# Where the softmax denominators of a head pair are transposed: from a PSUM bank of their own to the free block of the weights' bank, one step later

## The chip, the cores and the metric

The kernel runs on one core of a Trainium2 chip. The metric is the time of one execution on the device in microseconds (us). Engines work side by side, each in its own order: TensorE (PE in the profile; PEld is its weight load, which overlaps its matmuls), VectorE (DVE), ScalarE (ACT), GpSimd (POOL) and SyncE (SP, which here only issues DMAs; SPq is its queue). They wait for one another by semaphores. Matmuls and transposes on TensorE write to PSUM, which has eight banks of 128 partitions by 512 fp32 values; ScalarE and VectorE read them out.

## The reference

One layer of an encoder on 512 positions of width 1024, all in fp32:

```python
h = rms_norm(x, g1)
xr, gate, q, k, v = split(h @ w_in)
y_rnn  = (rg_lru(conv(xr), forward) + rg_lru(conv(xr), backward)) * gelu(gate)
y_attn = dilated_attention(q, k, v, rel_bias)     # 8 heads of 64
x = x + concat(rms_norm(y_rnn, ga), rms_norm(y_attn, gb)) @ w_out
x = x + square(relu(rms_norm(x, g2) @ w_up)) @ w_down
return rms_norm(x, g3)
```

The change is in `dilated_attention`. Each head looks at its keys through three windows (128 wide in steps of 1, 512 in steps of 4, 2048 in steps of 16), each with a softmax of its own, and the three outputs are combined by their denominators:

```python
lse = logsumexp(logits_w)                  # for each window w
out_w = softmax(logits_w) @ v
y = sum_w softmax_over_windows(lse)_w * out_w
```

This equals one softmax over the union of the keys, where a key that lies in several windows counts as often. So one sum of exponentials per query and head is enough, and the output is the weighted sum of values times the reciprocal of that sum, the denominator.

## The kernel before, in words

Matrix products are done in three passes with operands split into a high and a low part (`mm3`, lines 317 to 319). Weights stream in as chunks of 128 x 1024: a DMA brings a chunk to `wraw` (line 235), ScalarE makes the high part `whi` (line 252), VectorE the low part `wlo` (line 274), three chunks ahead of TensorE.

The positions are held by parity and half, in four query tiles of 128. Attention goes over four pairs of heads. The loop at line 1170 has five rounds, i = 0 to 4, of four steps, u = 0 to 3. In round i it computes the logits and exponentials of pair i (where i < 4), and transposes the exponentials of pair i - 1 (where i > 0). One step does, in this order on TensorE:

- `att_s` (line 815): the logits of one query tile for both heads of pair i, in two banks `ps` of the tag `gs` (four matmuls, line 824).
- `att_t` for both heads of pair i - 1 (line 857): three 128 x 128 transposes (line 862) of the exponentials `e` into one bank `pt`, of the tag `et`, which has two banks in turn; then ScalarE copies the three blocks to `ett` (line 865). A bank has room for four blocks. The key tile `jt` needs four query tiles, but of the fourth only 32 columns are inside the windows; `att_c` (line 867) does these on VectorE. The block left free in `pt` is block 0 for even `jt` and block 3 for odd `jt`. The step number u is the `jt` of the call.
- `att_e` (line 826), on VectorE and ScalarE: bias and row minimum (line 840), then the exponential with its sum (line 841), which adds up the denominators in `zz`.
- fillers: matmuls of the next projections (`pqk`) or of the output projection (`pwo`), in four places of a step, as `FILL` says.

When the four tiles of `ett` of a pair are there, `att_av` (line 961) multiplies them with the values into the bank `pav`, and line 976 multiplies by the reciprocal denominators `zrow`.

Those come in four parts. `att_z(i - 1)`, in step 0 of round i, takes the reciprocals on VectorE (line 892) and spreads each over 16 columns of a 128 x 128 tile `z16` (line 894; the profile names it `z`). `att_zt` (line 896), in the same step before the last place for fillers, transposes `z16` with TensorE into a bank `prow`, taken from the two banks of the tag `et` (line 898), and ScalarE copies it back over `z16` (line 899). `att_zd` (line 901), in step 1, after the second place for fillers, issues four DMAs from SP (line 906) that spread the rows of `z16` over `zrow`.

The order of the instructions on TensorE, ScalarE, VectorE and GpSimd is that of the program; this is set at line 112. SP is not in that list: the order of its DMAs, and which buffer of a tag a new tile gets, come from the planner that places the tiles. Tiles like `z16`, `ett`, `e` and `zrow` share one pool of 45 buffers (`g_`, line 118).

Of the kernel before, what the change touches and what calls it, by code (L numbers as in the profile page):

```python
# [14 lines left out]
AF = mybir.ActivationFunctionType  # L15
OP = mybir.AluOpType

P = 128
# [85 lines left out]
def hybrid_kernel(ctx: ExitStack, tc, xw0, xw, xn, w_in, w_v, w_out, w_up, w_dn, gates, vecs, rel, onehot, fg, out):  # L104
    nc = tc.nc
# [8 lines left out]
    act = nc.scalar.activation  # L114
# [3 lines left out]
    def g_(name, dt=FT, shape=(P, S)):  # L118
        return work.tile(list(shape), dt, name=name, tag="g", bufs=NG)
# [4 lines left out]
    def ps_(name, tag):  # L124
        return psum.tile([P, S], FT, name=name, tag=tag, bufs={"pj": 4, "gs": 2, "et": 2}[tag])
# [12 lines left out]
    ident = consts.tile([P, P], FT, name="ident")  # L138
# [268 lines left out]
    def fan(t, c, n, w):  # L407
        base = t[:, c:c + 1]
        return bass.AP(tensor=base.tensor, offset=base.offset, ap=[base.ap[0]] + ([[1, n]] if n > 1 else []) + [[0, w]])
# [77 lines left out]
    def load_tw(h, v):  # L487
        t = work.tile([P, 1024], FT, name="tw", tag="tw", bufs=4)[:, :2 * WN + TH + P]
        b = nbd.offset + h * 2 * S
        nc.sync.dma_start(t[:, WN:WN + TH + P], bass.AP(tensor=nbd.tensor, offset=b, ap=[[1, P], [1, TH + P]]))  # L490
        k = TH - WN - v
        nc.sync.dma_start(bass.AP(tensor=t.tensor, offset=t.offset, ap=[t.ap[0], [WN + TH + P, 2], [1, WN]]),
                          bass.AP(tensor=nbd.tensor, offset=b + S + k, ap=[[1, P], [P - 1 + v - k, 2], [1, WN]]))
        tws[h, v] = t
# [312 lines left out]
    et, en, zs = {}, {}, {}  # L807
# [7 lines left out]
    def att_s(p, u):  # L815
        qt = QSEQ[u]
        par, far = QT[qt]
        c0 = P * qt
        w = {(0, 0): TH + TH - WN, (0, 1): 0, (1, 0): TH - WN, (1, 1): TH}[par, far]
        psq[p] = [ps_("ps", "gs") for _ in range(2)]  # L820
        for e in range(2):
            k = k_tile(p, e)[:, w:w + NK]
            for i, n in enumerate(("h", "l")):
                nc.tensor.matmul(psq[p][e][:, :NK], lhsT=sp[p, 0, n, e][:, c0:c0 + P], rhs=k, start=i == 0, stop=i == 1)  # L824

    def att_e(p, u):
        qt = QSEQ[u]
        par, far = QT[qt]
        v = int(par != far)
        if u == 0:  # L830
            en[2 * p], en[2 * p + 1] = {}, {}
            zs[p] = small("zz", 8)
        pss = psq.pop(p)
        c0 = (WN + P) * far
        for e in range(2):
            h = 2 * p + e
            t = g_("e")
            mn = small("mn", 1)
            x = t[:, :NK] if far else t[:, S - NK:]
            nc.vector.tensor_tensor_reduce(x, pss[e][:, :NK], tws[h, v][:, c0:c0 + NK], 1.0, 3.0e38, OP.add, OP.min, mn)  # L840
            act(x, x, AF.Exp, scale=-1.0, bias=mn, accum_out=zs[p][:, 2 * qt + e:2 * qt + e + 1])
            en[h][qt] = t
            if u in (1, 3):
                del tws[h, v]
        if u == 3:
            for e in range(2):
                del sp[p, 0, "h", e], sp[p, 0, "l", e], sp[p, 1, "h", e]
            del kks[p]


    def blocks(jt):
        par, hj = jt // 2, jt % 2
        own = [(2 * (1 - par) + a, (P * hj if a else TH + P * hj)) for a in range(2)]
        oth = [(2 * par + a, (TH + P * hj if a else P * hj)) for a in range(2)]
        return (own + oth, slice(0, NK)) if hj else (oth + own, slice(S - NK, S))

    def att_t(h, jt):
        pt = ps_("pt", "et")
        bs = list(enumerate(blocks(jt)[0]))
        bs.pop(3 if jt % 2 else 0)  # L860
        for i, (qt, k) in bs:
            nc.tensor.transpose(pt[:, i * P:(i + 1) * P], en[h][qt][:, k:k + P], ident)  # L862
        t = et[h, jt] = g_("ett")
        c = slice(bs[0][0] * P, (bs[2][0] + 1) * P)
        act(t[:, c], pt[:, c], AF.Copy)

    def att_c(h, jt):
        hj = jt % 2
        qt = blocks(jt)[0][3 if hj else 0][0]
        c = slice(NK - 32, NK) if hj else slice(S - NK, S - NK + 32)  # L870
        nc.vector.transpose(et[h, jt][:, c], en[h][qt][:, c])
        if jt == 3:
            del en[h]
# [9 lines left out]

    pav, zrow = {}, {}

    z16 = {}

    def att_z(p):  # L890
        rz = small("rz", 8)
        nc.vector.reciprocal(rz, zs.pop(p))
        z16[p] = g_("z16")[:, :P]
        nc.vector.tensor_copy(z16[p], fan(rz, 0, 8, 16))

    def att_zt(p):
        pr = ps_("prow", "et")
        nc.tensor.transpose(pr[:, :P], z16[p], ident)
        act(z16[p], pr[:, :P], AF.Copy)

    def att_zd(p):
        zrow[p] = g_("zrow")
        t = z16.pop(p)
        for qt in range(4):
            r = t[32 * qt:32 * qt + 32]
            nc.sync.dma_start(zrow[p][:, qt * P:(qt + 1) * P],
                              bass.AP(tensor=r.tensor, offset=r.offset, ap=[r.ap[0], [0, 4], [1, P]]))

    def att_y(p):
        y_add(1)  # L910
# [50 lines left out]
    def att_av(p, jts):  # L961
        if 0 in jts:
            pav[p] = ps_("pav", "gs" if p else "pj")
        for jt in jts:
            parts = av_parts(jt)
            for i, (ci, co) in enumerate(parts):
                for e in range(2):
                    a = slice(64 * e, 64 * e + 64)
                    h = 2 * p + e
                    nc.tensor.matmul(pav[p][a, co], lhsT=vs[:, jt, h * DH:(h + 1) * DH], rhs=et[h, jt][:, ci],  # L970
                                     start=jt == 0 and i == 0, stop=jt == 3 and i == len(parts) - 1, skip_group_check=True)
            for e in range(2):
                del et[2 * p + e, jt]
        if 3 in jts:
            y = g_("yp")
            nc.vector.tensor_tensor(y[:, ::-1], pav.pop(p), zrow.pop(p), op=OP.mult)
            yat[p] = y
            if p == 3:
                att_a(p)
            if p != 2:  # L980
                att_q(p)
            if p < 2:
                att_a(p)
# [64 lines left out]
    def fill(n):  # L1048
        for _ in range(n):
            if fillers and fillers[0] is None:  # L1050
                fillers.popleft()
                load_x()
            if fillers:
                fillers.popleft()()
# [8 lines left out]
    def add_x():  # L1063
        for fn in more.popleft() if more else ():
            fn()
# [83 lines left out]
    def beside(*key):  # L1149
        for e in plan.pop(key, ()):  # L1150
            e()
# [18 lines left out]
    for i in range(5):  # L1170
        for u in range(4):
            if i < 4:
                att_s(i, u)
                if u == 2 and i < 3 or u == 0 and i:
                    for e in range(2):
                        load_tw(2 * (i + u // 2) + e, u // 2)
            if i >= 1:
                att_t(2 * i - 2, u)
                att_t(2 * i - 1, u)
            if i < 4:  # L1180
                att_e(i, u)
            if i >= 1:
                att_c(2 * i - 2, u)
                att_c(2 * i - 1, u)
            if u == 0 and i >= 1:
                att_z(i - 1)
            if u == 0:
                for p in AVS.get(i, ()):
                    att_av(p, range(4))
            beside(i, u, 0)  # L1190
            fill(FILL.get((i, u), (1, 1, 1, 1))[0])
            beside(i, u, 1)
            fill(FILL.get((i, u), (1, 1, 1, 1))[1])
            if u == 1 and i >= 1:
                att_zd(i - 1)
            if u == 0:
                for p in AVS.get(i, ()):
                    if p != 2:
                        att_y(p)
            beside(i, u, 2)  # L1200
            fill(FILL.get((i, u), (1, 1, 1, 1))[2])
            beside(i, u, 3)
            if u == 0 and i >= 1:
                att_zt(i - 1)
            fill(FILL.get((i, u), (1, 1, 1, 1))[3])
            add_x()
            beside(i, u, 4)
# [339 lines left out]
    for half in range(2):  # L1547
# [202 lines left out]
        if half == 1:  # L1750
# [27 lines left out]
            pr = ps_("pd", "pj")  # L1778
# [63 lines left out]
```

## Time and profile before

| | |
|---|---|
| median of 3 runs | 531.06 us (530.21 to 531.57) |
| the profiled execution: its time | 530.99 us |
| its span, first to last instruction | 528.9 us |
| mean granted TensorE clock | 0.998 |
| TensorE busy | 521.5 us, 99% of the span |
| VectorE, ScalarE busy | 437.5 us (83%), 357.2 us (68%) |
| attention rounds 1 to 4, from the trace | about 110 to 176 us of the span |

A row of the timeline gives the start in the span, the time from the first start to the last end of the instructions in the row, the engine, the source line, the operation with its output and inputs, the shape and the count; in brackets, how long the engine sat idle before it and what ended that. Matmuls overlap: the time that one takes from the engine is the distance of its start to the next one's start, not the duration in its row. The chain of waits gives this more directly: each row is the start, the time that the chain spent there, and on what. The list of waits gives engine, tile and line, what was waited for, and then the total, the number of times and the longest.

### The profile page before, as it was taken

To read this page: it belongs to the slowest core of one execution; us is meant where nothing else is said; L and a number is where in the kernel's file an instruction comes from. 1 tells how busy PE (TensorE), PEld (TensorE's weight loads), DVE (VectorE), ACT (ScalarE), POOL (GpSimd) and SP (SyncE) were. 2 spreads that over 40 slices of the span, in tenths; PEclk is the share of its full clock that TensorE was granted. 3 is DMA by queue.
4 is the path that set the end of the run, shared out by engine and by line. 5 is a ranking of instruction groups with operands and counts; after the bars stand their busy time and mean duration, and the time that the engine had idled before them with its cause. 6 is when DMAs were issued, how large, how long until landed. Compare 5 with 4: busy or idle time off the path is not lost.

```text
span 528.9 us, 8275 instructions
## 1 busy us (share of the span) xinstructions
PE 521.5 (99%) x3003; PEld 448.0 (85%) x3003; DVE 437.5 (83%) x672; ACT 357.2 (68%) x578; POOL 66.0 (12%) x89
## 2 busy tenths in 40 slices
PE   9999999999999999999999999999999999999995
PEld 7856888877887788899999888888999999888884
DVE  5999888987886888898779986879756988987885
ACT  6578947788865757586477755575566777655664
POOL 0272000000000041001200312001101210232000
PEclk9999999999999999999999999999999999999999
DMA  8654286587588289948395899986978397799704
GB/s 284 210 165 141 81 227 189 161 238 207 134 293 286 60 167 210 377 134 227 97 220 145 218 270 274 309 299 147 280 219 220 105 217 213 168 300 260 182 1 159
DMA packets 42600, 107.02 MB, mean 202 GB/s; under 512 B 4916, under 2 KB 15284, under 8 KB 42560
## 3 DMA queue, kind: packets, MB, share of 16 engines
q1 hardware_dynamic: 34848, 80.14, 46.1%
q0 software_dynamic: 7536, 26.14, 26.7%
q8 instruction: 23, 0.38, 0.3%
q10 hardware_dynamic: 176, 0.23, 0.1%
q14 instruction: 17, 0.14, 0.1%
HBM read 94.92 MB, written 4.23 MB: 187 GB/s over the span
## 4 chain that ended last, share of the span: by engine, by line
PE 96%; DMA 1%; DVE 1%; issue 1%; ACT 0%; SPq 0%; DVEq 0%; ACTq 0%
PE pu L317 10%; PE pu L318 10%; PE pu L319 10%; PE pd L317 10%; PE pd L318 10%; PE pd L319 10%; PE pwo L317 3%; PE pqk L317 3%; PE pwo L319 3%; PE pwo L318 3%; PE pqk L319 3%; PE pqk L318 3%; PE pav L970 2%; PE ps L824 2%; PE pt L862 2%; PE pv L317 2%
## 5 line engine op out<-in xcount | busy, mean ns | idle before, releaser
L274 DVE TENSOR_TENSOR wlo<-wraw,whi 128x1024 fp32r<-128x1024 f32 x71 | 86.7, 1221 | 24.5 <-ACT whi L252 24.2
L252 ACT ACTIVATE whi<-wraw 128x1024 fp32r<-128x1024 f32 x67 | 70.8, 1059 | 36.5 <-PE pd L319 19.3
L318 PE MATMUL pd<-wlo,ah 128*128 128x512 f32 (+1 forms) x195 | 75.2, 386 | 0.0
L317 PE MATMUL pd<-whi,ah 128*128 128x512 f32 (+1 forms) x195 | 75.2, 386 | 0.0
L319 PE MATMUL pd<-whi,al 128*128 128x512 f32 (+1 forms) x195 | 75.2, 386 | 0.0
L252 ACT ACTIVATE whi<-tw 128x1024 fp32r<-128x1024 f32 x38 | 40.2, 1059 | 40.7 <-DMA tw<-in_w_up_dram 12.9
L318 PE MATMUL pu<-hl,whi 128*128 128x256 f32 x224 | 63.4, 283 | 0.0
L319 PE MATMUL pu<-hh,wlo 128*128 128x256 f32 x224 | 63.4, 283 | 0.0
L317 PE MATMUL pu<-hh,whi 128*128 128x256 f32 x224 | 63.4, 283 | 0.0
L274 DVE TENSOR_TENSOR wlo<-tw,whi 128x1024 fp32r<-128x1024 f32 x38 | 46.4, 1221 | 18.7 <-ACT whi L252 18.6
L317 PE MATMUL pu<-h2h,whi 128*128 128x256 f32 (+1 forms) x200 | 60.1, 300 | 0.0
L318 PE MATMUL pu<-h2l,whi 128*128 128x256 f32 (+1 forms) x200 | 60.0, 300 | 0.0
L319 PE MATMUL pu<-h2h,wlo 128*128 128x256 f32 (+1 forms) x200 | 60.0, 300 | 0.0
L317 PEld LDWEIGHTS pu<-hh,whi 128*128 128x128 f32 x224 | 43.0, 192 | 0.0
L318 PEld LDWEIGHTS pu<-hl,whi 128*128 128x128 f32 x224 | 43.0, 192 | 0.0
L319 PEld LDWEIGHTS pu<-hh,wlo 128*128 128x128 f32 x224 | 43.0, 192 | 0.0
L319 PEld LDWEIGHTS pd<-whi,al 128*128 128x128 f32 x195 | 36.6, 188 | 7.4
L317 PEld LDWEIGHTS pd<-whi,ah 128*128 128x128 f32 x195 | 36.6, 188 | 7.3
L318 PEld LDWEIGHTS pd<-wlo,ah 128*128 128x128 f32 x195 | 36.6, 188 | 7.3
L252 ACT ACTIVATE whi<-ts 128x1024 fp32r<-128x1024 f32 x24 | 25.5, 1061 | 23.9 <-PE pd L319 18.1
L317 PEld LDWEIGHTS pu<-h2h,whi 128*128 128x128 f32 x200 | 38.3, 191 | 1.3
L319 PEld LDWEIGHTS pu<-h2h,wlo 128*128 128x128 f32 x200 | 38.3, 191 | 1.3
(282 smaller groups left out, 1250.3 us busy)
## 6 DMA issues: line engine op xcount, KB each, us to landing
wraw<-in_w_up_dram SPq DMA_DIRECT2D x25, 512.0 KB, 5.5
ts<-in_w_dn_dram POOLq DMA_DIRECT2D x24, 512.0 KB, 13.3
wraw<-in_w_dn_dram SPq DMA_DIRECT2D x24, 512.0 KB, 7.1
tw<-in_w_up_dram SPq DMA_DIRECT2D x15, 512.0 KB, 5.4
tw<-in_w_up_dram POOLq DMA_DIRECT2D x15, 512.0 KB, 8.4
wraw<-in_w_in_dram SPq DMA_DIRECT2D x13, 512.0 KB, 3.6
ts<-in_w_dn_dram SPq DMA_DIRECT2D x8, 512.0 KB, 6.6
tw<-in_w_dn_dram SPq DMA_DIRECT2D x8, 512.0 KB, 6.1
```

Of the source, the lines that this page charges most:

```text
L252: act(hi, raws[i], AF.Copy)
L274: nc.vector.tensor_tensor(lo, r, f(splits[i][0]), op=OP.subtract)
L317: nc.tensor.matmul(o, lhsT=a[0], rhs=b[0], start=bool(first), stop=False, skip_group_check=on)
L318: nc.tensor.matmul(o, lhsT=a[0], rhs=b[1], start=False, stop=False, skip_group_check=on)
L319: nc.tensor.matmul(o, lhsT=a[1], rhs=b[0], start=False, stop=bool(last), skip_group_check=on)
L824: nc.tensor.matmul(psq[p][e][:, :NK], lhsT=sp[p, 0, n, e][:, c0:c0 + P], rhs=k, start=i == 0, stop=i == 1)
L862: nc.tensor.transpose(pt[:, i * P:(i + 1) * P], en[h][qt][:, k:k + P], ident)
L970: nc.tensor.matmul(pav[p][a, co], lhsT=vs[:, jt, h * DH:(h + 1) * DH], rhs=et[h, jt][:, ci], start=jt == 0 and i == 0, stop=jt == 3 and i ...
```

## The change

`att_zt` and its call go. In `att_t`, for the first head of the pair (`h % 2 == 0`) and `jt == 1`, the tile `z16` of this pair is transposed into block 3 of `pt`, after the three blocks of exponentials; after ScalarE's copy of the three blocks, a second copy takes block 3 back to `z16`. That is the first `att_t` of step 1 in place of the end of step 0. `att_z` and `att_zd` stay where they are in the program.

```diff
+    z16 = {}
+
     def att_t(h, jt):
         pt = ps_("pt", "et")
         bs = list(enumerate(blocks(jt)[0]))
         bs.pop(3 if jt % 2 else 0)
+        z = z16[h // 2] if (h % 2, jt) == (0, 1) else None
         for i, (qt, k) in bs:
             nc.tensor.transpose(pt[:, i * P:(i + 1) * P], en[h][qt][:, k:k + P], ident)
+        if z is not None:
+            nc.tensor.transpose(pt[:, 3 * P:], z, ident)
         t = et[h, jt] = g_("ett")
         c = slice(bs[0][0] * P, (bs[2][0] + 1) * P)
         act(t[:, c], pt[:, c], AF.Copy)
+        if z is not None:
+            act(z, pt[:, 3 * P:], AF.Copy)
...
-    def att_zt(p):
-        pr = ps_("prow", "et")
-        nc.tensor.transpose(pr[:, :P], z16[p], ident)
-        act(z16[p], pr[:, :P], AF.Copy)
...
             beside(i, u, 3)
-            if u == 0 and i >= 1:
-                att_zt(i - 1)
             fill(FILL.get((i, u), (1, 1, 1, 1))[3])
```

More of the change, by code (lines that the diff above doesn't have):

```diff
@@ L884, in hybrid_kernel @@
     pav, zrow = {}, {}
-    z16 = {}
     def att_z(p):
```

## The prediction

> **What bounds the kernel now.** I read the page first (busy shares, clock, the chain by engine), then TensorE's list of waits, then the four places where the lone transpose stands, in the timeline and in the chain of waits, and last the queues beside them.
>
> ```profile
> span 528.9 us, 8275 instructions
> PE 521.5 (99%) x3003; PEld 448.0 (85%) x3003; DVE 437.5 (83%) x672; ACT 357.2 (68%) x578; POOL 66.0 (12%) x89
> ...
> PE 96%; DMA 1%; DVE 1%; issue 1%; ACT 0%; SPq 0%; DVEq 0%; ACTq 0%
> ```
>
> TensorE is the bound: busy for 99% of the span, 96% of the chain. Time on another engine counts only where TensorE then waits. Little of its time is waiting, but two entries of its list belong to the step that is moved:
>
> ```profile
> PEld prow L898 <- issue: 0.8, 1, 0.8
> ...
> PEld pt L862 <- ACT z L899: 0.6, 2, 0.3
> ```
>
> The first is the lone transpose in one round: TensorE stands before it. The second is twice a batch of `pt` transposes that waits until ScalarE has read `prow`, since that tile took one of the two `et` banks out of turn.
>
> **The change part by part.** Counts do not change: four transposes of `z` and four copies of 128 x 128 go, four of each come; reciprocals and the 16 DMAs stay. What counts is where they stand.
>
> *The transpose itself.* Its price on the path, alone (rounds 2, 3, 4) and in a batch of six (round 2), from the chain of waits:
>
> ```profile
> 134.87 0.11 PE prow L898
> ...
> 136.43 0.65 PE pt L862 x6
> ...
> 151.73 0.11 PE prow L898
> ...
> 170.29 0.11 PE prow L898
> ```
>
> Alone it takes 0.11 us; in a batch 0.65 / 6 = 0.11. So moving it gains and costs nothing by itself: 4 x (0.11 - 0.11) = 0.
>
> *The wait in round 1.* TensorE and VectorE there, then two later batches for comparison:
>
> ```profile
> 113.21 0.40 PE L319 MATMUL pqk<-h_hi,wlo 128*128 128x512 f32 x1
> 113.95 0.30 PE L898 MATMUL prow<-ident,z 128*128 128x128 f32 x1 [0.35 <-DVE z L894]
> 114.01 0.48 PE L317 MATMUL pqk<-h_hi,whi 128*128 128x512 f32 x1
> 114.33 0.39 PE L318 MATMUL pqk<-h_lo,whi 128*128 128x512 f32 x1
> 114.56 0.39 PE L319 MATMUL pqk<-h_hi,wlo 128*128 128x512 f32 x1
> ...
> 115.55 1.08 PE L862 MATMUL pt<-ident,e 128*128 128x128 f32 x6
> ...
> 112.65 0.59 DVE L840 CUSTOM_DVE_ANT_0 e<-ps,tw 128x416 f32<-128x416 f32 x1 [1.29 <-issue]
> ...
> 113.58 0.23 DVE L894 COPY z<-rz 128x128 f32<-128x128 f32 x1
> ...
> 136.27 0.82 PE L862 MATMUL pt<-ident,e 128*128 128x128 f32 x6
> ...
> 170.24 1.08 PE L862 MATMUL pt<-ident,e 128*128 128x128 f32 x6
> ```
>
> Starts of these matmuls are 0.23 apart (114.33 to 114.56). From L319 at 113.21 to L318 at 114.33 are 1.12; two steps without the transpose are 0.46; the lone transpose thus costs 0.66 here, 0.11 its own and 0.55 waiting. VectorE idled 1.29 and so finished `z` at 113.81. After the change TensorE goes on with L317 at 113.44 and comes to `z` only inside the next batch, which stands at 115.55 now and would start 0.66 earlier, at 114.89: 1.08 after `z` is written. The wait goes: 0.55.
>
> *The bank.* The batch at 115.55 lasts 1.08, that of round 2 without a wait 0.82: 0.26 of waiting for `prow` to be read. At 170.24, in round 4, again 1.08: 0.26. With no tile `prow`, the two heads keep to their banks, both read a step earlier: 0.52 goes.
>
> Sum: 0.55 + 0.26 + 0.26 = 1.07 off the path.
>
> *What is late next: ScalarE.* Its copies of `z` move behind the first `ett` copy and push the second one and two exponentials back by 0.28 us; what follows the old place comes that much earlier. Nothing on TensorE reads these exponentials before the next round. VectorE hardly moves in round 1, so TensorE, 0.81 earlier (0.55 + 0.26), meets the last exponentials of the round at their old time:
>
> ```profile
> 126.94 0.64 ACT L841 ACTIVATE e<-e,mn 128x416 f32<-128x416 f32 x1
> ...
> 128.19 0.77 PEld L862 LDWEIGHTS pt<-ident,e 128*128 128x128 f32 x6
> ```
>
> These are ready at 127.58. The second head's loads begin after three of six, about 128.60; 0.81 earlier is 127.79, still 0.2 later. Cost 0; if that cover goes, at most what ScalarE loses beyond 0.2, which the 0.28 of the copy bounds: 0.1.
>
> The copy of the three blocks may have to wait for the fourth transpose as well, since that writes the same bank: 0.11 later on ScalarE in each round, beside which TensorE does the second head's batch, so nothing on the path; if TensorE had no such cover, 4 x 0.11 = 0.44. The Trainium skill, "PSUM — Partial Sum Buffer", section "PSUM bank collisions raise a hardware error", has the stricter form, against this change: TensorE may not write a bank while ScalarE reads it. By that the wait is certain and not a chance; no row of before shows a bank so shared, and the sum stays.
>
> *The DMAs of `zrow`, and SP.* `zrow` is needed only at the end of the next `pav`, but its buffers matter at the end of round 3:
>
> ```profile
> 151.88 0.28 ACT L899 ACTIVATE z<-prow 128x128 f32<-128x128 f32 x1 [0.41 <-PE prow L898]
> 152.96 0.88 ACT L865 ACTIVATE ett<-pt 128x384 f32<-128x384 f32 x2 [0.81 <-PE pt L862]
> ...
> 153.72 2.75 SPq L906 DMA_DIRECT2D zrow<-z  x4
> 156.81 3.06 SPq L1078 DMA_DIRECT2D x<-in_xn_dram  x4
> ...
> 160.69 0.88 ACT L865 ACTIVATE ett<-pt 128x384 f32<-128x384 f32 x2 [2.12 <-DMA zrow<-z]
> ...
> 162.07 0.64 ACT L841 ACTIVATE e<-e,mn 128x416 f32<-128x416 f32 x1
> ...
> 162.59 0.81 PEld L862 LDWEIGHTS pt<-ident,e 128*128 128x128 f32 x6
> ```
>
> ScalarE waits 2.12 for `zrow` to land, then come the exponentials that end at 162.71; the second head's loads need them at about 163.04. Slack 0.33. `z` is copied at 152.16 now; then, the copy stands after the first `ett` copy, which ends at about 152.96 + 0.44 + 0.11 - 0.81 = 152.70, so `z` is there at 152.98, before SP's place at 153.72 and, if SP too comes 0.5 to 0.8 earlier, about when it gets there. TensorE comes 0.81 earlier, so it stalls if this chain comes less than 0.81 - 0.33 = 0.48 earlier. Bounds: 0 if the chain follows TensorE, 0.48 if the DMAs stay where they are. SP's work before it is released mostly by VectorE and by landings, and both follow TensorE in rounds 2 and 3; I take 0.1, near the lower end.
>
> In round 4 the copy of `z` is the only thing SP waits for:
>
> ```profile
> 170.44 0.28 ACT L899 ACTIVATE z<-prow 128x128 f32<-128x128 f32 x1 [1.20 <-PE prow L898]
> ...
> 176.11 2.96 PE pav L970 x24
> ```
>
> It moves behind one `ett` copy of 0.5, against 0.81 gained: the same moment within 0.3, and `pav`'s end, which reads `zrow`, is eight microseconds off. Cost 0. After 176 us TensorE hardly waits, and the weight DMAs behind it are released by the buffers it frees, so what is gained by then stays.
>
> So 1.07 - 0.1 = about 0.97. The profiled execution took 530.99 for a span of 528.9 (2.09 around it) and the median is 531.06, 0.07 more: 531.06 - 0.97 = 530.1.
>
> **The rivals.**
> (a) The chain at the end of round 3, or the exponentials of round 1, do not follow, and the wait goes on there. Price: 0.48 + 0.1 of the 1.07; time 531.06 - 0.49 = 530.6. For it: the slacks of 0.33 and 0.2. Against it: SP's place comes after `z`.
> (b) Slower: `zrow` goes later in SP's queue. SP's order is not the program's, and it has been turned at this very place:
>
> ```profile
> 137.31 0.44 SPq L492 DMA_DIRECT2D tw<-nbd  x1
> 137.85 0.42 SPq L490 DMA_DIRECT2D tw<-nbd  x1
> 138.37 1.11 SPq L803 DMA_DIRECT2D ql<-ql  x2
> 139.57 2.55 SPq L906 DMA_DIRECT2D zrow<-z  x4
> ```
>
> The program issues L490 and L492 in pairs, yet the partner of the second L490 is not behind it. A planner that holds `z` to be ready later may put the four `x` loads of 156.81 ahead of `zrow` in round 3. Price: their 3.06 less the slack 0.33 = 2.73 of stall; 531.06 - 1.07 + 2.73 = 532.7. It decides from a lateness of 1.07 + 0.33 = 1.40. Against it: the call of the DMAs keeps its place, and `z` still comes first in time.
> (c) More than the sum: the lone transpose is dearer than the chain's 0.11, as the start distances around it would show if TensorE drained on the change of operand. Its matmul took 0.27 to 0.30 in the row; at 0.27 for the part that batching hides, 4 x (0.27 - 0.11) = 0.64 more, 531.06 - 1.07 - 0.64 = 529.4. "TensorE: Matmul & The Clock Gate" of the Trainium skill, Part 4, has about 275 ns for a transpose within a kernel, the same length. Against it: rounds 2 to 4 give 0.11 three times. Another placing of buffers that ends the wait on `zrow` would come out here too.
>
> **How the numbers follow.** Within 0.3% (1.6 us) is about what a measurement of this kernel can tell from no change; the runs shown spread over 1.36. Chances: forecast 0.53, (a) 0.12, (b) 0.15, (c) 0.20. The predicted time is the forecast's, 530.1; its own range is 529.5 to 530.7. Below 529.47 lie most of (c) and a tail of the forecast: faster 0.25. Above 532.65 lies most of (b): slower 0.13. The rest is 0.62. The range goes from (c) less half of the runs' spread, 528.8, to (b), 532.7.
>
> **What would show it.** Right: no `prow` of `z`; no wait of `z` on TensorE in round 1; the batches of step 1 with seven transposes, the first of four, lasting about 0.82 + 0.11 = 0.93 in all four rounds; `pav` of round 4 ending about 1 us earlier; `ett` copies of the first head 0.11 later after their batch. Wrong: a wait before the batch that opens round 2 or round 4 (a), `zrow` behind other DMAs in round 3 and exponentials late (b), start distances around the old places of rounds 2 to 4 that shrink by more than 0.11 (c).

## The result and the profile after

The changed kernel takes 529.34 us (median of 12 runs, 528.73 to 530.92) against 530.62 us for the kernel before (12 runs, 529.43 to 532.71). The ratio is 0.9974 with a 95% interval of 0.9962 to 0.9986: 1.4 us less, between 0.7 and 2.0. It is taken over all executions, not from the medians, which differ by 1.28. The profiled execution has a span of 527.0 us against 528.9.

That difference of 1.9 us is not the change's alone, and the chain of waits shows how much of it is. Its rows for the batches of `pt`, first of the kernel before (start, time on the path, what):

```profile
110.86 0.67 PE pt L862 x6
...
120.15 0.66 PE pt L862 x6
...
140.60 0.66 PE pt L862 x6
...
162.98 0.66 PE pt L862 x6
...
172.71 0.66 PE pt L862 x6
```

and the same batches of the kernel after (`z` is line 867 now):

```profile
110.11 0.65 PE pt L865 x6
...
114.28 0.33 PE pt L865 x3
114.61 0.11 PE pt L867
114.72 0.33 PE pt L865 x3
...
118.54 0.66 PE pt L865 x6
...
138.94 0.66 PE pt L865 x6
...
161.30 0.66 PE pt L865 x6
...
168.61 0.33 PE pt L865 x3
168.94 0.11 PE pt L867
169.05 0.33 PE pt L865 x3
...
170.76 0.66 PE pt L865 x6
```

The first row of each is the batch that opens round 1, ahead of anything that was changed, and it already stands 0.75 us earlier (110.86 to 110.11). From there on, distances tell, not positions:

| stretch between starts of batches | before, us | after, us | difference |
|---|---|---|---|
| round 1, step 0 to step 2 | 9.29 | 8.43 | -0.86 |
| round 1, step 2 to round 2, step 2 | 20.45 | 20.40 | -0.05 |
| round 2, step 2 to round 4, step 0 | 22.38 | 22.36 | -0.02 |
| round 4, step 0 to step 2 | 9.73 | 9.46 | -0.27 |
| all of it | 61.85 | 60.65 | -1.20 |

From the last of these batches to the end of the span it is the same in both: 528.9 - 172.71 = 356.19 before, 527.0 - 170.76 = 356.24 after. So the change itself is worth 1.20 us in this pair of profiles, 1.13 of it in the two places where TensorE used to wait for the moved step; the other 0.7 is where round 1 happened to begin.

In TensorE's list of waits the two entries of the kernel before are gone; what stands there of the attention, beside entries put down to the issue, is this:

```profile
PEld ps L824 <- DMA ql<-ql: 0.6, 1, 0.6
...
PEld pav L968 <- DVE ett L878: 0.4, 1, 0.4
```

The first lies ahead of round 1's first batch and came to 0.3 in the kernel before. The second, at the start of the last `pav`, is new in name only: the load there stood idle for 0.36 before as well, put down to the issue.

### The profile page after: what moved, and what is told of

The parts are those of the page before. It is cut to its first block, busy times and chain, and to the rows that moved or that the text cites. A ratio compares the mean times of both kernels' runs of the same rounds, so it can differ in the third digit from the quotient of the medians.

```text
span 527.0 us, 8277 instructions
## 1 busy us (share of the span) xinstructions
PE 519.9 (99%) x3003; PEld 448.5 (85%) x3003; DVE 437.4 (83%) x672; ACT 356.6 (68%) x578; POOL 65.9 (13%) x89
## 4 chain that ended last, share of the span: by engine, by line
PE 86%; DVE 5%; ACT 4%; issue 2%; DMA 2%; ACTq 0%; SPq 0%; DVEq 0%
PE pu L318 10%; PE pu L317 10%; PE pu L319 10%; PE pd L317 10%; PE pd L319 10%; PE pd L318 10%; PE pwo L317 3%; PE pwo L319 3%; PE pwo L318 3%; PE pav L968 2%; PE pt L865 2%; DMA ql<-ql 2%; PE ps L824 2%; PE pg L538 1%; PE pqk L317 1%
## 5 line engine op out<-in xcount | busy, mean ns | idle before, releaser
L318 PEld LDWEIGHTS pu<-h2l,whi 128*128 128x128 f32 x200 | 38.3, 192 | 1.3
```

The lines of the kernel that those rows point to most:

```text
L318: nc.tensor.matmul(o, lhsT=a[0], rhs=b[1], start=False, stop=False, skip_group_check=on)
```

## Experiments

The stretch from the first batch of round 1 to the third of round 4, which is 61.85 us before, is the measure below, beside the times. A few tenths of a us are resolved by it, and they are not by the times, whose intervals are mostly 0.1 to 0.2% (0.6 to 1 us) to either side.

**The changed kernel once more.**

> The changed kernel as it is, beside the three experiments below. The theory: three waits of TensorE go (0.55 us for z in round 1, 0.26 for the bank in rounds 1 and 4), so the stretch from the first batch of round 1 to the third batch of round 4 is 1.0 to 1.2 us shorter than 61.85 us, and the time about 1.1 us (0.2%) less. The rival, that more than the waits went (start of the program, planner): the stretch shorter by 1.5 us or more, time 1.6 us less.

Measured: 529.29 us against 530.85, ratio 0.9977 (0.9965 to 0.9989). The stretch is 172.17 - 111.44 = 60.73 us, 1.12 less than before:

```profile
111.44 0.66 PE pt L865 x6
...
162.60 0.75 PE pt L865 x6
...
172.17 0.65 PE pt L865 x6
```

The span of this execution is 529.0 us, 0.1 longer than that of the kernel before, since round 1 begins at 111.44 and 0.6 us more of it went behind the stretch (529.0 - 172.17 = 356.83), where TensorE's list of waits has an entry that neither the kernel before nor the first profile of the changed one has (at about 490 us):

```profile
PEld pd L317 <- issue: 0.6, 1, 0.6
```

So the rival has no support: a span of 527.0 was a matter of the execution, and 1.1 to 1.2 us is what belongs to the change.

**Later, but still in a bank of the same two.**

```diff
-            if u == 0 and i >= 1:
-                att_zt(i - 1)
             fill(FILL.get((i, u), (1, 1, 1, 1))[3])
+            if u == 0 and i >= 1:
+                att_zt(i - 1)
```

> The kernel before, with the lone transpose one place of fillers later (0.69 us of matmuls in rounds 1 and 2; rounds 3 and 4 have no filler there), still in its own bank of the tag et. The theory says that the wait for z goes and comes back at the bank: ScalarE now makes whi (1.06 us) before it reads prow, so the second head's transposes of step 1 wait until about 1.0 us later than before in round 1, and 0.1 to 1.0 us in round 2: slower by 1.1 to 2.0 us. The rival, that the wait for z alone is what the change saves: faster by 0.55 us. The rival that the lone transpose is dear: no difference.

Measured: 532.79 us, ratio 1.0034 (1.0022 to 1.0046), stretch 63.48 us (110.47 to 173.95), 1.63 longer than before. TensorE's weight loads for the second head in step 1 of round 1, first in the kernel before, then in this kernel in rounds 1 and 2, and the chain of waits ahead of the first of these two:

```profile
116.08 0.31 PEld L862 LDWEIGHTS pt<-ident,e 128*128 128x128 f32 x3 [0.28 <-ACT z L899]
```

```profile
116.51 0.31 PEld L862 LDWEIGHTS pt<-ident,e 128*128 128x128 f32 x3 [1.69 <-ACT z L899]
...
137.81 0.31 PEld L862 LDWEIGHTS pt<-ident,e 128*128 128x128 f32 x3 [0.91 <-ACT z L899]
```

```profile
114.58 0.64 ACT qh L789
...
115.23 1.06 ACT whi L252
116.29 0.17 ACT z L899
```

The wait for `z` is gone, and the wait for the bank has grown from 0.28 to 1.69 in round 1 and from nothing to 0.91 in round 2. The matmuls that now come first bring their `whi` conversion with them, 1.06 us on ScalarE ahead of the copy that frees the bank. The sum agrees: 1.69 - 0.28 - 0.55 = 0.86 in round 1 and 0.91 in round 2 make 1.77, against 1.63 measured. So a later place alone loses: the wait for `z` is not all that the moved step cost, and the bank is a part of it.

**At the old place, in another set of banks.**

```diff
     def att_zt(p):
-        pr = ps_("prow", "et")
+        pr = ps_("prow", "pj")
```

> The kernel before, with prow of the denominators in the tag pj (four banks) in place of et, at its old place. The theory: both bank waits go, the wait for z in round 1 stays at 0.55 us or so: faster by 0.52 us, stretch 61.3 us. The rival that the lone transpose is dear: no difference. The rival that the wait for z is all: no difference.

Measured: 530.30 us, ratio 0.9994 (0.9982 to 1.0006): not told from no change, and not from -0.52 us either. The stretch is 174.31 - 113.07 = 61.24, 0.61 less than before. The chain of waits in round 1 of this kernel:

```profile
113.07 0.67 PE pt L862 x6
...
115.85 0.24 DVE z L894
...
116.14 0.33 PE prow L898
...
117.93 0.66 PE pt L862 x6
...
172.27 0.66 PE pt L862 x6
```

The batches of step 1 in rounds 1 and 4 take 0.66 and wait for no bank, while the chain still runs through VectorE's `z` to the lone transpose. Of the 0.61, 0.26 is gained in steps 0 and 1 of round 1 (113.07 to 122.10, 9.03 for 9.29) and 0.28 in those of round 4 (164.86 to 174.31, 9.45 for 9.73): the two bank waits, and little else. This profile is also the plainest case of how little a span says here: round 1 begins at 113.07, mostly because of this entry ahead of everything, at the start of the program, which came to 0.5 in the kernel before:

```profile
PEld pxr L448 <- ACT h_hi L358: 2.2, 1, 2.2
```

**Later and in another set of banks.** Both edits together: alone in a bank of its own, waiting for nothing.

> The kernel before, with the lone transpose one place later and in the tag pj: alone, in a bank of its own, but waiting for nothing. The theory: all three waits go, 1.07 us, the same time as the changed kernel within 0.2 us, and a stretch of about 60.7 us. The rival that a lone transpose is dearer than one in a batch: slower than the changed kernel by up to 0.64 us.

Measured: 529.76 us, ratio 0.9989 (0.9975 to 1.0002). The stretch is 172.05 - 110.62 = 61.43, only 0.42 less than before, where 60.7 was expected. Round 1 did gain (12.65 us from its first to its last batch, 13.48 before, 12.61 in the changed kernel); the rest was lost at one place. ScalarE at the end of round 3, and TensorE's loads of the batch that opens round 4:

```profile
160.63 0.87 ACT L865 ACTIVATE ett<-pt 128x384 f32<-128x384 f32 x2 [2.28 <-DMA zrow<-z]
```

```profile
162.17 0.31 PEld L862 LDWEIGHTS pt<-ident,e 128*128 128x128 f32 x3 [0.52 <-ACT e L841]
162.79 0.20 PEld L862 LDWEIGHTS pt<-ident,e 128*128 128x128 f32 x2 [0.31 <-ACT e L841]
```

The landing of `zrow` held the `ett` copy, this held the exponentials, and TensorE's loads waited 0.83 us for them: rival (a) of the prediction at its place, in a kernel where the lone transpose itself takes 0.11 in the chain. The dearer lone transpose, rival (c), would have shown in all rounds. Two runs tell whether the landing is chance, and whether it is the cause.

> The same kernel as r4_later_other_bank, for a second look. There the three waits went, but TensorE waited 0.8 us for exponentials at the start of round 4, behind the landing of zrow. If that is a matter of the DMAs' chance, the wait is shorter or absent here and the stretch nearer 60.7 us; if it belongs to the kernel, it is 0.5 to 0.8 us again and the stretch 61.2 to 61.5 us.

Measured: 530.00 us, ratio 0.9999 (0.9981 to 1.0017). The stretch is 171.75 - 111.02 = 60.73, and the batch that opens round 4 waits for nothing:

```profile
111.02 0.65 PE pt L862 x6
...
162.29 0.66 PE pt L862 x6
...
171.75 0.66 PE pt L862 x6
```

The queue of SP and the `ett` copy, first in r4, then in r5:

```profile
152.86 2.92 SPq L906 DMA_DIRECT2D zrow<-z  x4
```

```profile
153.28 2.77 SPq L906 DMA_DIRECT2D zrow<-z  x4
...
160.22 0.87 ACT L865 ACTIVATE ett<-pt 128x384 f32<-128x384 f32 x2 [2.34 <-DMA zrow<-z]
```

Counted from round 1's first batch, the four DMAs are issued at the same place (42.24 and 42.26 us), and the copy that waits for them begins at 50.01 and 49.20. The same program, 0.70 us less in the same stretch: chance of the DMAs. (The ratio of 0.9999, beside a median 0.9 below that of the kernel before, is drawn up by long executions, the longest of 534.58 us.)

**The coupling cut.** That `ett` copy waits for the four DMAs of `zrow`; the theory is that its buffer is the one that `z16` held. A buffer of its own for `z16` should then take that wait away:

```diff
-        z16[p] = g_("z16")[:, :P]
+        z16[p] = work.tile([P, P], FT, name="z16", tag="z16", bufs=1)
```

> r4_later_other_bank with the tile z16 in a buffer of its own instead of the pool of 45, so that the first ett copy of step 3 in round 3 no longer waits for the DMAs of zrow. The theory that r4 lost its gain to that landing: the wait at the start of round 4 goes, stretch 60.6 to 60.8 us, as the changed kernel. The rival that a lone transpose costs more than one in a batch: no wait there, and the stretch still 0.4 us or more above the changed kernel's.

> The changed kernel with the tile z16 in a buffer of its own. If the landing of zrow still costs it a little in some executions (0.09 us in its second profile), that goes: stretch 60.6 us, time 0 to 0.3 us below the changed kernel. The rival, that the new place of all the later tiles in the pool costs something: slower by some tenths.

Measured on the kernel of r4: 529.95 us, ratio 0.9990 (0.9973 to 1.0008), stretch 171.29 - 110.53 = 60.76. On the changed kernel: 529.68 us, ratio 0.9983 (0.9971 to 0.9995), stretch 171.06 - 110.41 = 60.65. The `ett` copy at the end of round 3, first in r6, then in r7:

```profile
158.83 0.87 ACT L865 ACTIVATE ett<-pt 128x384 f32<-128x384 f32 x2 [1.43 <-PE pt L862]
```

```profile
158.61 0.87 ACT L870 ACTIVATE ett<-pt 128x384 f32<-128x384 f32 x2 [1.43 <-PE pt L865]
```

It follows TensorE's batch now and no DMA, so the theory holds. The changed kernel itself still has this wait, which its profile hides:

```profile
159.34 0.88 ACT L870 ACTIVATE ett<-pt 128x384 f32<-128x384 f32 x2 [2.22 <-PE pwo L319]
...
159.66 0.31 DVE L878 STREAM_TRANSPOSE ett<-e 128x32 f32<-128x32 f32 x2 [1.01 <-DMA zrow<-z]
```

The first row names a matmul of `pwo` that happened to end nearby, but in the trace's semaphore events the last of the four DMAs lands 0.23 to 0.24 us ahead of this copy in both profiles of the changed kernel, as in the kernel before, in r4 and in r5. The stretches of r5, r6, r7 and the changed kernel lie within 0.11 us: once nothing waits, it makes no difference that shows whether `z` is transposed alone in a bank of its own or in the free block. A buffer of its own for `z16` brought no gain in time that shows either.

**The price of a lone transpose.** On the changed kernel:

```diff
+    def alone(i, u, n):
+        if 1 <= i <= 3:
+            if n == 0:
+                lone["p"] = ps_("plone", "pj")
+            nc.tensor.transpose(lone["p"][:, n * P:(n + 1) * P], ident, ident)
...
+            alone(i, u, 0)
             fill(FILL.get((i, u), (1, 1, 1, 1))[0])
...
```

and so ahead of each of the four fillers of a step.

> The changed kernel with 48 more transposes of the identity, one ahead of each place of fillers in rounds 1 to 3, into a bank of the tag pj that nobody reads: four per step, 36 of them between matmuls of 512 columns or ahead of the logits, 12 right behind the batch of the step. At 0.11 us each, 48 add 5.3 us: stretch 65.9 us. At 0.27 us each, as the rival has it, 13 us: stretch 73.6 us.

Measured: 535.27 us, ratio to the kernel before 1.0101 (1.0072 to 1.0130). The stretch is 177.09 - 110.98 = 66.11 us, 5.46 more than the changed kernel's: 5.46 / 48 = 0.114 us each, and nowhere near the 13 us of the rival. In the chain of this kernel:

```profile
116.95 0.23 PE pqk L319
117.18 0.11 PE plone L1153
117.29 0.23 PE pqk L317
```

## Why the prediction was right

The time forecast was 530.1 us against a median of 531.06, a gain of 0.97. Measured, the gain is 1.4 us (0.7 to 2.0) by the runs and 1.12 to 1.20 by the stretch in two profiles. The mechanism was right, and the profiles put the sum of the waits at 0.05 to 0.13 above the 1.07. The time itself says less: 529.34 us lies 0.8 below the forecast, just outside the forecast's own range of 529.5 to 530.7 and next to the 529.4 of rival (c), which r8 refutes. Of the 0.8, 0.44 is that the kernel before measured 530.62 over twelve runs and not 531.06 over three, which is chance. The lower end of the wider range is also off by a slip of 0.1 (529.4 less half of 1.36 is 528.7, not 528.8); nothing hangs on it.

*The transpose itself, 0.* Right: 0.11 in the batch (rows of line 867), 0.114 alone (r8). Rival (c) has fallen. The row's duration of 0.27 us is not what a transpose takes from TensorE, and with it falls the reading of the Trainium skill's 275 ns ("TensorE: Matmul & The Clock Gate", Part 4) as a price on the path. That figure agrees with the duration.

*The wait in round 1 and the banks, 0.55 + 0.26 + 0.26.* Right in place and size: 0.86 in round 1 for 0.81, 0.27 in round 4 for 0.26. That the waits for `z` and for the bank are separate is shown by the experiments. Other banks at the old place (r3) took 0.61 out of the stretch for 0.52. The later place on top of that (r5 and r6, which lack the wait of r4) took out another 0.48 to 0.51, which is the wait for `z`, for 0.55. A later place in the same banks (r2) put 1.63 in.

*ScalarE, no cost.* Right. The batch that opens round 2, where the cover was 0.2 us, waits for no exponentials in the changed kernel:

```profile
126.91 0.65 PE pt L865 x6
```

The first `ett` copy does wait for the fourth transpose; step 1 of round 3, before and after:

```profile
152.44 0.81 PE L862 MATMUL pt<-ident,e 128*128 128x128 f32 x6
```

```profile
150.64 0.49 PE L865 MATMUL pt<-ident,e 128*128 128x128 f32 x3
...
151.07 0.49 PE L865 MATMUL pt<-ident,e 128*128 128x128 f32 x3
...
151.27 0.49 ACT L870 ACTIVATE ett<-pt 128x384 f32<-128x384 f32 x1 [1.49 <-PE pt L867]
```

The copy begins 0.63 after the batch, 0.52 before (152.44 to 152.96): the 0.11 that was forecast, and TensorE did not wait for it. The batch of seven lasts 0.92 (150.64 to 151.56) for the 0.93 forecast. The wait agrees with what the Trainium skill states in "PSUM — Partial Sum Buffer" ("PSUM bank collisions raise a hardware error"), that TensorE and ScalarE may not access one bank in the same partition at once. What would happen without the wait, no run here shows.

*The end of round 3, 0.1 between 0 and 0.48.* The chain was right, the bounds were too narrow. The changed kernel lost 0 in one profile (batch 0.66) and 0.09 in the other (0.75), but the kernel of r4, with the same chain, lost 0.70 against r5. The step that failed is the upper end, "if the DMAs stay where they are": it took the landing of `zrow` as fixed or earlier, and it moves by itself from execution to execution. The `ett` copy that waits for it began 49.83 us after round 1's first batch in the kernel before (160.69 less 110.86), and 50.01 in r4, 49.20 in r5, with one program. With a landing 0.18 later than before, the prediction's own sum gives 0.81 + 0.18 - 0.33 = 0.66 of stall, close to the 0.70. That the changed kernel lost so little in its two profiles (49.23 and 49.31) is therefore partly luck.

*SP's order, rival (b).* Did not come: in the queue of the changed kernel, `zrow` in round 3 stands where it stood, ahead of the four `x` loads:

```profile
152.66 2.69 SPq L904 DMA_DIRECT2D zrow<-z  x4
155.55 3.00 SPq L1076 DMA_DIRECT2D x<-in_xn_dram  x4
```

What stays open: the kernels with the lone transpose that waits for nothing (r4 to r6) have medians 0.9 to 1.1 us below that of the kernel before, the changed kernel and r7 1.2 to 1.6. The intervals overlap and the stretches do not show it, so nothing is made of it here.

## What to carry to other kernels

When the matmul engine is busy 99% of the time, look in its list of waits for the small steps that use a bank out of turn: such a step can cost twice, once when it waits for its input and once when the next user waits for its reader (here in one and in two of four rounds), and moving it later without giving it another bank only moved the wait (here from 0.28 to 1.69 us). A free block of a bank that is taken anyway, at a later place, took both waits away; a bank from a set with more of them, at the later place, did as well. To judge a gain of 0.2%, compare distances between the same instructions around the change, not spans: what comes before it can shift by more than the gain.

## What was not expected of the hardware

The position of round 1 in the span moved between 110.11 and 113.07 us in ten profiles of kernels whose source is the same up to that point, 3 us against a change worth 1.2. Most of it arises at the start of the program: the transposes of line 414 begin at 23.4 us in the earliest of the ten and at 26.2 in the latest. Ahead of them TensorE waits for what ScalarE makes of the first loaded tiles (2.2 us in r3, 0.5 in the kernel before). The landing of four small DMAs, issued at the same place, moved by 0.8 us between two executions of one program, and where a buffer's reuse hangs on it, this comes out on the matmul engine in one execution and not in the next.
